# Part 3 of the MLP: its second matrix computed plainly instead of with seven products

## The chip, the cores and the metric

The kernel runs on one core of one Trainium2 chip. The metric is device time in microseconds (us), from the first instruction to the last; a lower number is better. The core has five engines that run side by side, each through its own queue in order: TensorE (PE in the rows; PEld is its loading of the stationary operand), VectorE (DVE), ScalarE (ACT), GpSimd (POOL) and SyncE (SP), which here only issues transfers. TensorE writes its sums into eight accumulators ("banks") of 128 x 512 numbers.

## The reference

Two layers work on 512 tokens of 1024 channels. Each layer has a mixer (sparse attention, gated linear attention and pooling side by side), a normalisation, the MLP and a second normalisation. Only the last two are touched:

```
D_MODEL, SEQ, D_FF = 1024, 512, 4096
for l in range(2):
    ...
    h = layer_norm(ALPHA * h + mixed @ w_out[l], ln1_g[l], ln1_b[l])
    ff = square(relu(h @ w_up[l])) @ w_down[l]
    h = layer_norm(ALPHA * h + ff, ln2_g[l], ln2_b[l])
```

All data are float32.

## The kernel before

**Precision.** A product of two float32 matrices is made of three matmuls: each operand is split into a high part (a copy that rounds, by ScalarE) and a low part (operand minus high part, by VectorE), and high x high, high x low and low x high are summed in one bank (`steps`, line 598). A weight tile of 128 x 1024 numbers is loaded by SyncE into a raw buffer (four of them, `NRAW`, and two more for "chained" tiles), then split into one of four pairs of buffers (`NSPL`, lines 385 to 443). A pair becomes free when the last matmul that reads it is done.

**The MLP in four parts.** `mlp` (line 1716) goes through the 4096 hidden channels in four parts `c` of 1024. In each part the first matrix makes 512 x 1024 activations, squares of relu, which are split into high and low; the second matrix multiplies them with 1024 rows of `w_down` and adds the result to `h`, four tiles of 128 tokens x 1024 channels. Part 0 does both plainly. Its second matrix is a loop over two halves of 512 output columns, over four pairs of weight rows j, over four token tiles t (lines 1770 to 1783): each weight tile is used by all four token tiles, then released, and four banks are open. It is 2 x 4 x 4 x 2 x 3 = 192 matmuls of 512 columns.

**Seven products.** In parts 1 to 3 both matrices are cut into quarters, and seven products of sums of quarters take the place of eight. For the first matrix this is `up_pair` (line 1519): pairs of 128-channel blocks, matmuls of 256 columns. For the second it is `down_seven` (line 1667), in the order of `STEPS` (line 1856). The activation quarters are A11, A12, A21, A22: the first digit is the half of the tokens, the second the even or odd block of 128 hidden channels. The sums S1 to S4 of activation quarters are made by `sums` (line 1592) on VectorE and split by `split_sums` (line 1652). The sums of weight quarters are made by transfers that add to a raw buffer, issued on GpSimd's queue (`accumulate`, line 358; eight in each part), each after the split of the sum before it (`group`, line 419). One part's second matrix is 7 products x 2 token tiles x 2 x 2 weight rows x 3 = 168 matmuls of 512 columns. Some products end in one bank and are added to `h` more than once: `out` (line 1673) adds a bank to a half of a token tile.

**What follows part 3.** When both halves of a token tile have had their last addition (and its statistics, `bn_stats`), `norm` (line 562) normalises it: aggregate on VectorE (mv), two small steps on GpSimd (rs, the reciprocal root), two passes with mv and two with rs on VectorE. In layer 0 TensorE then transposes the tile in two groups of four (`transpose_h`, line 536), ScalarE and VectorE split the result into hT, and layer 1 begins with block A, 96 matmuls of 400 columns, token tile by token tile, and block B. In layer 1 the normalised halves are transferred out.

**The order.** A planner in the kernel (`Planner`, line 35) writes out every engine's order before the program runs: it follows estimated costs (`pl.op`, `pl.pe`), lets one main generator issue matmuls and takes spawned generators (splits, additions, normalisations, transposes) as soon as its own clock says that what they need is ready. The chip then runs each queue in exactly that order.

Of the kernel before, what the change touches and what calls it, by code (L numbers as in the profile page):

```python
# [130 lines left out]
def trunk_kernel(ctx: ExitStack, tc, x, w_in, cmp_pos, cmp_w1, cmp_w2, gla_w_gate2, gla_b_gate,  # L131
# [151 lines left out]
    for l in range(depth):  # L283
# [36 lines left out]
        for c in range(4):  # L320
# [11 lines left out]
            if c == 0:  # L332
                dn = [[add_unit((2, 512), [(full, cols(w_down[l], 8 * c + 2 * j, 2, 512 * hf, 512))])
                       for j in range(4)] for hf in range(2)]
            else:
                dn = quarters(w_down[l], c)
# [302 lines left out]
    def layer_work(l, hT, nhT):  # L639
# [879 lines left out]
        def up_pair(i0, i1, ff, m, c):  # L1519
# [63 lines left out]
            def out12():  # L1583
# [6 lines left out]
                pl.spawn(sums(), 1)  # L1590
# [76 lines left out]
        def down_seven(ff, dn, c, stat):  # L1667
# [3 lines left out]
            seen = []  # L1671

            def out(n, number, i, t, hf, op, end, fin):
# [5 lines left out]
                if fin and c == 3:  # L1679
                    yield  # L1680
                    nc.vector.bn_stats(stat[t][:, hf, :], h[t][:, s])  # L1681
                    pl.op("dve", 0.6, [stat[t]], [h[t]])
                    seen.append(t)
                    if seen.count(t) == 2:
                        pl.spawn(norm(l + 1, t, stat[t], gb2, None if last else nhT), 1)
# [4 lines left out]
            for (name, src, n, _), (f, b, outs) in zip(SEVEN, STEPS):  # L1690
# [3 lines left out]
                t0, hf, op, end, fin = outs  # L1694
# [5 lines left out]
                for i, j in order:  # L1700
# [10 lines left out]
                    if j == 1:  # L1711
                        pl.spawn(out(b, count[b], i, t0 + i, hf, op, end, fin), 1)
# [3 lines left out]
        def mlp():  # L1716
            for c in range(4):
# [18 lines left out]
                else:  # L1736
                    ff = {n: [None] * 4 for n in ("A11", "A12", "A22", "S1", "S2", "S3", "S4", "raw")}
                    pl.spawn(split_sums(ff, c, 0), 3)
                    yield from up_pairs(up, ff, c)

                def ff_ready(k, t):
                    return E("ff", id(ffp[t // 2]), k // 2)

                def ff_parts(k, t):
                    c0 = 256 * (k % 2) + 128 * (t % 2)
# [15 lines left out]
                def done(ps, t, hf):  # L1761
                    y_part(ps, t, slice(512 * hf, 512 * hf + 512), True)
                    yield

                if c == 3:
                    drop(12)
                if c:
                    yield from down_seven(ff, dn, c, stat)
                    continue
                for hf in range(2):  # L1770
                    if True:
                        pss = []
                        for j in range(4):
                            for t in range(NT):
# [4 lines left out]
                                piece(pss[t], t, dn[hf][j], j)  # L1779
# [47 lines left out]
    def everything():  # L1827
# [3 lines left out]
        for l in range(depth):  # L1831
# [24 lines left out]
STEPS = (("A11", "e", (0, 0, OP.add, False, False)), ("S1", "b", (2, 1, OP.add, False, False)),  # L1856
         ("S2", "e", (0, 1, OP.subtract, False, False)), ("S4", "b", (0, 1, OP.add, True, True)),
# [59 lines left out]
```

## Time and profile before

| | us |
|---|---|
| median of 3 runs | 1214.7 |
| lowest, highest | 1212.32, 1216.29 |
| the profiled execution | 1213.42 |
| its span, first to last instruction | 1211.7 |
| TensorE busy | 1169.2 (96%) |
| VectorE busy | 1009.7 (83%) |
| ScalarE busy | 666.8 (55%) |
| GpSimd busy | 238.4 (20%) |
| mean granted clock of TensorE | 0.988 of full |

Times in the rows are counted from the start of the span. A matmul's end is modelled and overlaps the next one's start, so the distance of two starts is what one costs, not its length. A wait is put down to the engine and line that came last.

### The profile page before, as it was taken

To read this page: it belongs to the slowest core of one execution; us is meant where nothing else is said; L and a number is where in the kernel's file an instruction comes from. 1 tells how busy PE (TensorE), PEld (TensorE's weight loads), DVE (VectorE), ACT (ScalarE), POOL (GpSimd) and SP (SyncE) were. 2 spreads that over 40 slices of the span, in tenths; PEclk is the share of its full clock that TensorE was granted. 3 is DMA by queue.
4 is the path that set the end of the run, shared out by engine and by line. 5 is a ranking of instruction groups with operands and counts; after the bars stand their busy time and mean duration, and the time that the engine had idled before them with its cause. 6 is when DMAs were issued, how large, how long until landed. Compare 5 with 4: busy or idle time off the path is not lost.

```text
span 1211.7 us, 19153 instructions
## 1 busy us (share of the span) xinstructions
PE 1169.2 (96%) x7161; PEld 1025.5 (85%) x7161; DVE 1009.7 (83%) x1810; ACT 666.8 (55%) x1299; POOL 238.4 (20%) x301
## 2 busy tenths in 40 slices
PE   8999999999999999999899999999999999999995
PEld 7898788889889899797688987888998898988974
DVE  3799998897679799797867999988967897987978
ACT  4633666663348567386336435756633584774851
POOL 1255431210001201102212644302100011011021
PEclk9999999999999999999989998999999999999998
DMA  7514103153325836747634040131523358466482
GB/s 217 148 40 118 44 19 109 27 152 105 88 76 151 168 111 127 151 140 156 136 97 116 22 134 29 36 96 35 158 87 104 105 122 157 140 113 157 147 158 88
DMA packets 138317, 132.80 MB, mean 110 GB/s; under 512 B 17744, under 2 KB 104304, under 8 KB 138224
## 3 DMA queue, kind: packets, MB, share of 16 engines
q1 hardware_dynamic: 125168, 106.41, 29.6%
q0 software_dynamic: 13056, 25.17, 12.6%
q8 instruction: 56, 0.92, 0.3%
q14 instruction: 37, 0.30, 0.1%
HBM read 129.46 MB, written 2.10 MB: 109 GB/s over the span
## 4 chain that ended last, share of the span: by engine, by line
PE 67%; DVE 17%; DMA 8%; issue 4%; ACT 2%; POOL 2%; SPq 0%; DVEq 0%; POOLq 0%; ACTq 0%
PE b L181 64%; DMA wr<-in_w_down_dram 7%; DVE s L206 6%; DVE wl L206 3%; PE b L186 3%; DVE s L219 2%; DVE h L219 1%; DVE nb L223 1%; ACT s L194 1%; ACT wh L194 1%; DVE h L206 1%; POOL s L206 1%; POOL r L206 1%; DMA h<-in_x_dram 1%; DVE stats L1681 1%
## 5 line engine op out<-in xcount | busy, mean ns | idle before, releaser
L181 PE MATMUL b<-wh,s 128*128 128x512 f32 x1184 | 386.7, 399 | 5.1 <-DVE mv L564 2.2
L194 ACT ACTIVATE wh<-wr 128x1024 fp32r<-128x1024 f32 (+4 forms) x230 | 220.3, 969 | 217.2 <-PE b L181 126.7
L206 DVE TENSOR_TENSOR wl<-wr,wh 128x1024 fp32r<-128x1024 f32 (+4 forms) x222 | 251.8, 1140 | 96.5 <-ACT wh L194 95.6
L181 PEld LDWEIGHTS b<-wh,s 128*128 128x128 f32 x1184 | 222.9, 189 | 59.9 <-ACT wh L194 4.0
L194 ACT ACTIVATE s<-s 128x512 fp32r<-128x512 f32 (+7 forms) x424 | 216.0, 534 | 96.7 <-DVE s L206 75.8
L181 PE MATMUL b<-wl,s 128*128 128x512 f32 x592 | 234.6, 396 | 4.1 <-DVE wl L206 4.1
L194 ACT ACTIVATE s<-b 128x384 fp32r<-128x384 f32 (+6 forms) x270 | 121.4, 460 | 142.3 <-PE b L181 102.3
L206 DVE TENSOR_TENSOR s<-s,s 128x512 fp32r<-128x512 f32 (+6 forms) x302 | 183.7, 627 | 13.3 <-ACT s L194 7.1
L181 PE MATMUL b<-hTh,wh 128*128 128x256 f32 (+1 forms) x544 | 176.7, 325 | 3.1 <-ACT s L194 3.1
L181 PE MATMUL b<-hTh,wl 128*128 128x256 f32 (+1 forms) x544 | 174.6, 321 | 0.0
L181 PE MATMUL b<-hTl,wh 128*128 128x256 f32 (+1 forms) x544 | 174.2, 320 | 0.0
L360 POOL DMA_DIRECT2D wr<-in_w_down_dram x48 | 58.3, 1237 | 547.2 <-DVE wl L206 321.0
L181 PE MATMUL b<-s,s 128*128 128x256 f32 (+4 forms) x1008 | 143.7, 296 | 0.0
L181 PEld LDWEIGHTS b<-wl,s 128*128 128x128 f32 x592 | 111.7, 189 | 30.6 <-DVE wl L206 6.8
L181 PEld LDWEIGHTS b<-s,s 128*128 128x128 f32 (+1 forms) x1008 | 125.0, 191 | 2.3 <-issue 0.3
L206 DVE TENSOR_TENSOR s<-b,s 128x256 f32<-128x256 f32 (+8 forms) x206 | 100.4, 499 | 20.3 <-PE b L181 12.5
L181 PEld LDWEIGHTS b<-hTh,wh 128*128 128x128 f32 x544 | 102.5, 188 | 12.4 <-ACT s L194 4.3
L181 PEld LDWEIGHTS b<-hTh,wl 128*128 128x128 f32 x544 | 102.6, 189 | 8.5
L181 PEld LDWEIGHTS b<-hTl,wh 128*128 128x128 f32 x544 | 102.5, 189 | 8.1
L181 PE MATMUL b<-hTh,s 128*128 128x256 f32 x576 | 108.9, 283 | 0.0
L181 PEld LDWEIGHTS b<-hTh,s 128*128 128x128 f32 x576 | 91.7, 191 | 0.1
L181 PE MATMUL b<-hTl,s 128*128 128x256 f32 x288 | 81.4, 283 | 0.0
(151 smaller groups left out, 1686.6 us busy)
## 6 DMA issues: line engine op xcount, KB each, us to landing
wr<-in_w_up_dram SPq DMA_DIRECT2D x52, 512.0 KB, 4.4
wr<-in_w_down_dram SPq DMA_DIRECT2D x52, 512.0 KB, 4.4
wr<-in_w_down_dram POOLq DMA_DIRECT2D x48, 512.0 KB, 5.9
wr<-in_w_out_dram SPq DMA_DIRECT2D x20, 512.0 KB, 3.5
wr<-in_w_in_dram SPq DMA_DIRECT2D x24, 384.0 KB, 3.2
wr<-in_w_up_dram SPq DMA_DIRECT2D x24, 256.0 KB, 3.2
wr<-in_w_in_dram SPq DMA_DIRECT2D x8, 400.0 KB, 6.2
wr<-in_w_in_dram SPq DMA_DIRECT2D x6, 512.0 KB, 3.6
```

The source lines that it names most:

```text
L181: nc.tensor.matmul(o, a, b, start=start, stop=stop, **({"skip_group_check": True} if loose else {}))
L186: nc.tensor.transpose(o, a, i)
L194: nc.scalar.activation(o, a, func, scale=scale, **kw)
L206: e.tensor_tensor(out=o, in0=a, in1=b, op=op)
L219: nc.vector.scalar_tensor_tensor(o, a, s, b, op0=op0, op1=op1)
L223: nc.vector.tensor_reduce(o, a, axis=AX.X, op=op, negate=negate)
L360: nc.gpsimd.dma_start(o, a, accum_op=OP.add)
L1681: nc.vector.bn_stats(stat[t][:, hf, :], h[t][:, s])
```

## The change

In part 3 alone, of both layers, the second matrix is computed as in part 0, with 192 matmuls instead of 168; parts 1 and 2 keep the seven products, and the first matrix of part 3 does too. The eight weight tiles of part 3 are loaded and split as they are: no tile is "chained", and no transfer adds to one. Of the activations the quarter A21 itself is kept and split (in `out12`), and their sums are not made. The first half of the output columns goes pair of weight rows by pair of weight rows over four open banks, as in part 0. The second half goes token tile by token tile: tile t takes all four weight tiles one after the other, so all four stay in the split buffers until tile 3 has used them. Behind each tile of the second half comes its normalisation at once (`done`). The additions to `h` carry the statistics in part 3.

```diff
--- before.py
+++ after.py
@@ -329,7 +329,7 @@
                     up.append([add_unit((8, 128), [(full, cols(w_up[l], 0, 8, 1024 * c + 128 * m, 128))])])
                     if c and m % 2:
                         pairs[up[-1][0]] = up[-2][0]
-            if c == 0:
+            if c in (0, 3):
                 dn = [[add_unit((2, 512), [(full, cols(w_down[l], 8 * c + 2 * j, 2, 512 * hf, 512))])
                        for j in range(4)] for hf in range(2)]
             else:
@@ -1587,7 +1587,16 @@
                 yield
                 act(x_, x_, AF.Relu)
                 act(x_, x_, AF.Square)
-                pl.spawn(sums(), 1)
+                if c < 3:
+                    pl.spawn(sums(), 1)
+                    return
+                f = slot(dt=F32R)
+                act(f[:, lo_], x_)
+                yield
+                tt(f[:, hi_], x_, f[:, lo_], OP.subtract)
+                ff["A21"][m // 2] = f[:, lo_], f[:, hi_]
+                drop(3)
+                ev("ff", c, "A21", m // 2)
 
             def sums():
                 yield [key("C11"), key("X1")]
@@ -1664,25 +1673,17 @@
                     ff[n][p] = fh[:, s_], fl[:, s_]
                     ev("ff", c, n, p)
 
-        def down_seven(ff, dn, c, stat):
+        def down_seven(ff, dn, c):
 
 
             ps = {}
-            seen = []
-
-            def out(n, number, i, t, hf, op, end, fin):
+
+            def out(n, number, i, t, hf, op, end):
                 s = slice(512 * hf, 512 * hf + 512)
                 tt(h[t][:, s], h[t][:, s], ps[n][i], op)
                 if end:
                     free()
                 ev("down", c, n, number, i)
-                if fin and c == 3:
-                    yield
-                    nc.vector.bn_stats(stat[t][:, hf, :], h[t][:, s])
-                    pl.op("dve", 0.6, [stat[t]], [h[t]])
-                    seen.append(t)
-                    if seen.count(t) == 2:
-                        pl.spawn(norm(l + 1, t, stat[t], gb2, None if last else nhT), 1)
                 yield
 
             count = {"a": 0, "b": 0, "e": 0}
@@ -1691,7 +1692,7 @@
                 if not count[b]:
                     yield [("bank", 2)]
                     ps[b] = [bank(), bank()]
-                t0, hf, op, end, fin = outs
+                t0, hf, op, end = outs
                 keys = [(dn[src][j], n) for j in range(2)]
                 if f in ("A12", "S3", "A22"):
                     order = [(i, j) for i in range(2) for j in range(2)]
@@ -1709,7 +1710,7 @@
                     if i == 1:
                         used(keys[j])
                     if j == 1:
-                        pl.spawn(out(b, count[b], i, t0 + i, hf, op, end, fin), 1)
+                        pl.spawn(out(b, count[b], i, t0 + i, hf, op, end), 1)
                 drop({"A11": 4, "S1": 0, "S2": 8, "S3": 8, "S4": 0, "A12": 0, "A22": 8}[f])
                 count[b] += 1
 
@@ -1734,14 +1735,22 @@
                         yield from early_up(m, 1, ffp, acc)
                     ev("upped")
                 else:
-                    ff = {n: [None] * 4 for n in ("A11", "A12", "A22", "S1", "S2", "S3", "S4", "raw")}
-                    pl.spawn(split_sums(ff, c, 0), 3)
+                    ff = {n: [None] * 4 for n in ("A11", "A12", "A21", "A22", "S1", "S2", "S3", "S4", "raw")}
+                    if c < 3:
+                        pl.spawn(split_sums(ff, c, 0), 3)
                     yield from up_pairs(up, ff, c)
 
+                def quarter(k, t):
+                    return "A" + "12"[t // 2] + "12"[k % 2]
+
                 def ff_ready(k, t):
+                    if c:
+                        return E("ff", c, quarter(k, t), k // 2)
                     return E("ff", id(ffp[t // 2]), k // 2)
 
                 def ff_parts(k, t):
+                    if c:
+                        return [a[:, 128 * (t % 2):128 * (t % 2) + 128] for a in ff[quarter(k, t)][k // 2]]
                     c0 = 256 * (k % 2) + 128 * (t % 2)
                     return [a[:, c0:c0 + 128] for a in ffp[t // 2][k // 2]]
 
@@ -1758,17 +1767,37 @@
                         a, b = ff_parts(k, t)
                         passes(ps, a, b, wh[:, kk, :], wl[:, kk, :], k == 0, k == 7)
 
-                def done(ps, t, hf):
-                    y_part(ps, t, slice(512 * hf, 512 * hf + 512), True)
+                def done(ps, t, hf, c=c, stat=stat):
+                    y_part(ps, t, slice(512 * hf, 512 * hf + 512), c == 0, stat[t][:, hf, :] if c == 3 else None)
                     yield
+                    if c == 3 and hf == 1:
+                        yield from norm(l + 1, t, stat[t], gb2, None if last else nhT)
 
                 if c == 3:
                     drop(12)
-                if c:
-                    yield from down_seven(ff, dn, c, stat)
+                if c in (1, 2):
+                    yield from down_seven(ff, dn, c)
                     continue
+
+                def piece_steps(ps, t, ui, j):
+                    wh, wl = parts[ui]
+                    for kk in range(2):
+                        k = 2 * j + kk
+                        a, b = ff_parts(k, t)
+                        yield from steps(ps, a, b, wh[:, kk, :], wl[:, kk, :], k == 0, k == 7)
+
                 for hf in range(2):
-                    if True:
+                    if c == 3 and hf == 1:
+                        for t in range(NT):
+                            yield [("bank", 1)]
+                            ps = bank()
+                            for j in range(4):
+                                yield [("split", dn[hf][j])]
+                                yield from piece_steps(ps, t, dn[hf][j], j)
+                                if t == NT - 1:
+                                    used(dn[hf][j])
+                            pl.spawn(done(ps, t, hf), 1)
+                    else:
                         pss = []
                         for j in range(4):
                             for t in range(NT):
@@ -1776,7 +1805,10 @@
                                 if j == 0:
                                     yield [("bank", 1)]
                                     pss.append(bank())
-                                piece(pss[t], t, dn[hf][j], j)
+                                if c:
+                                    yield from piece_steps(pss[t], t, dn[hf][j], j)
+                                else:
+                                    piece(pss[t], t, dn[hf][j], j)
                                 if j == 3:
                                     pl.spawn(done(pss[t], t, hf), 2)
                             used(dn[hf][j])
@@ -1853,10 +1885,10 @@
 LAND = 5.5
 SEVEN = (("P1", "B11", 0, False), ("P5", "B11", 1, False), ("P6", "B11", 2, False), ("P3", "B22", 0, False),
          ("P2", "B21", 0, True), ("P7", "B22", 1, True), ("P4", "B11", 3, True))
-STEPS = (("A11", "e", (0, 0, OP.add, False, False)), ("S1", "b", (2, 1, OP.add, False, False)),
-         ("S2", "e", (0, 1, OP.subtract, False, False)), ("S4", "b", (0, 1, OP.add, True, True)),
-         ("A12", "a", (0, 0, OP.add, True, True)), ("S3", "e", (2, 1, OP.subtract, False, True)),
-         ("A22", "e", (2, 0, OP.add, True, True)))
+STEPS = (("A11", "e", (0, 0, OP.add, False)), ("S1", "b", (2, 1, OP.add, False)),
+         ("S2", "e", (0, 1, OP.subtract, False)), ("S4", "b", (0, 1, OP.add, True)),
+         ("A12", "a", (0, 0, OP.add, True)), ("S3", "e", (2, 1, OP.subtract, False)),
+         ("A22", "e", (2, 0, OP.add, True)))
 NATT = (6, 8)
 NEARLY = 2
 KEEP = 6
```

## Rows read from the trace of the kernel before

**Rows 1.** The page, part 1: busy time, share and instructions of TensorE.

```profile
PE 1169.2 (96%) x7161; PEld 1025.5 (85%) x7161; DVE 1009.7 (83%) x1810; ACT 666.8 (55%) x1299; POOL 238.4 (20%) x301
```

**Rows 2.** TensorE timeline (start, length, instruction): part 0's plain stage and what follows.

```profile
309.31 0.40 PE L181 MATMUL b<-wh,s 128*128 128x512 f32 x1
...
353.97 0.28 PE L181 MATMUL b<-hTh,wh 128*128 128x256 f32 x1
```

**Rows 3.** TensorE timeline, layer 0: part 3's seven products, first and last.

```profile
555.75 0.39 PE L181 MATMUL b<-wh,s 128*128 128x512 f32 x1
...
602.39 0.39 PE L181 MATMUL b<-wh,s 128*128 128x512 f32 x1
```

**Rows 4.** TensorE's waits, 555 to 603 us: releaser, total, times, longest.

```profile
PE b L181 <- DVE wl L206: 1.8, 2, 1.0
PE b L181 <- DVE mv L564: 1.5, 1, 1.5
PE b L181 <- ACT s L194: 0.8, 1, 0.8
PE b L181 <- DVE s L206: 0.5, 1, 0.5
```

**Rows 5.** TensorE timeline, layer 1: part 0's start, part 3's first and last.

```profile
910.45 0.40 PE L181 MATMUL b<-wh,s 128*128 128x512 f32 x1
...
1156.59 0.40 PE L181 MATMUL b<-wh,s 128*128 128x512 f32 x1
...
1199.09 0.39 PE L181 MATMUL b<-wh,s 128*128 128x512 f32 x1
```

**Rows 6.** TensorE timeline between the layers: tile 0's transposes, block B's start.

```profile
603.68 0.66 PE L186 MATMUL b<-ident,h 128*128 128x128 f32 x4 [0.91 <-DVE h L219]
607.48 1.11 PE L186 MATMUL b<-ident,h 128*128 128x128 f32 x4 [3.15 <-DVE h L219]
...
631.20 0.40 PE L181 MATMUL b<-hTh,wh 128*128 128x512 f32 x1
```

**Rows 7.** One stretch: length, busy us of five engines, granted clock, DMA, GB/s.

```profile
608.20:612.40 4.20, 4.05 (x14) 3.40 (x13) 4.20 (x7) 1.00 (x2) 1.52 (x2) 0.50 0.24 63
```

**Rows 8.** TensorE timeline, block A of layer 1: transposes, matmuls.

```profile
614.77 0.60 PE L186 MATMUL b<-ident,h 128*128 128x128 f32 x4
...
615.40 0.34 PE L181 MATMUL b<-wl,hTh 128*128 128x400 f32 x1
...
618.85 0.34 PE L181 MATMUL b<-wh,hTh 128*128 128x400 f32 x1
...
623.60 0.34 PE L181 MATMUL b<-wh,hTl 128*128 128x400 f32 x1
```

**Rows 9.** Timeline of VectorE behind layer 1's last matmul.

```profile
1200.58 0.64 DVE L206 TENSOR_TENSOR h<-h,b 128x512 f32<-128x512 f32 x1
...
1201.80 0.69 DVE L1681 BATCH_NORM_STATS2 stats<-h 128x6 f32<-128x512 f32 x1
...
1203.05 0.20 DVE L564 BATCH_NORM_AGGREGATE mv<-stats 128x2 f32<-128x12 f32 x1
...
1205.78 1.41 DVE L219 SCALAR_TENSOR_TENSOR h<-h,mv,s 128x512 f32<-128x512 f32 x2
1207.10 1.41 DVE L219 SCALAR_TENSOR_TENSOR h<-h,rs,s 128x512 f32<-128x512 f32 x2
```

**Rows 10.** Timeline of VectorE, layer 0: splits of 1024 columns in parts 0 and 3.

```profile
332.93 1.23 DVE L206 TENSOR_TENSOR wl<-wr,wh 128x1024 fp32r<-128x1024 f32 x1 [0.17 <-ACT wh L194]
...
592.68 1.18 DVE L206 TENSOR_TENSOR wl<-wr,wh 128x1024 fp32r<-128x1024 f32 x1
```

**Rows 11.** Timeline of GpSimd: steps of the reciprocal root, layer 0 and layer 1.

```profile
592.87 1.08 POOL L212 TENSOR_SCALAR rs<-mv 128x1 f32<-128x1 f32 x1 [14.46 <-DVE mv L564]
...
1200.76 0.22 POOL L212 TENSOR_SCALAR rs<-mv 128x1 f32<-128x1 f32 x1 [5.77 <-DVE mv L564]
...
1204.03 0.92 POOL L206 TENSOR_TENSOR rs<-rs,mhalf 128x1 f32<-128x1 f32 x1
```

## The prediction

> **What bounds the kernel now.** TensorE is busy in 96% of the span [rows 1], and nearly all of it at one matmul after the other, so the first question of any change here is how many matmuls it adds and how many gaps it closes. The share alone can't answer that; the places can. I looked at the order of TensorE's work in three kinds of stretch, then at its waits in them, then at VectorE after the last matmul.
>
> Plain second matrix, as part 0 has it: the 192 matmuls of 512 columns of layer 0 begin at 309.31 and the next stage begins at 353.97 [rows 2]: 44.66 us, 0.2326 us each, with no wait listed between. That is the pitch of this matmul when nothing holds it.
>
> Seven products, as part 3 has it: the stage holds 7 x 2 x 2 x 2 x 3 = 168 matmuls of the same form, 39.1 us at that pitch. In layer 0 it runs from 555.75 to 602.39 + 0.23 = 602.62 [rows 3], 46.9 us: 7.8 us are lost. The waits there [rows 4] add up to 4.6 us and have four causes: the split of a weight sum that is late, an accumulator that is not yet taken up, and sums of activations that ScalarE and VectorE still make (the row that names mv stands behind the addition to h that frees the accumulator). The rest is lower pace behind those waits. In layer 1 the same 168 run from 1156.59 to 1199.09 + 0.23 [rows 5], 42.7 us: 3.6 us lost.
>
> Behind the stage of layer 0 comes the normalisation of all four token tiles, their transposes and block A of layer 1 (96 matmuls of 400 columns). The reader is to see the two gaps before transposes that wait for the normalised tile, 0.91 and 3.15 us, that block A comes only behind the second, and that block B starts at 631.20 [rows 6]: 28.6 us from the last matmul of part 3. [...] At full pace block A's matmuls are (623.60 - 618.85) / 26 = 0.183 us apart, and a group of four transposes adds 615.40 - 614.77 - 0.18 = 0.45 us [rows 8]. So the work there is 96 x 0.183 + 8 x 0.45 = 21.1 us, and I allow 0.3 us for the small transposes of the parameters: 21.4. 7.2 us of the 28.6 are lost.
>
> Behind the stage of layer 1 comes only VectorE: it finishes at 1207.10 + 1.41 = 1208.51 [rows 9], 9.4 us after the start of the last matmul, because the tails of tiles 0 to 3 lie on it one behind the other.
>
> **The change, part by part.** All sums are against the profiled execution, 1213.42 us with a span of 1211.7; the median of the runs shown is 1214.7, 1.3 above it, and I carry the difference over to the median.
>
> Matmuls. 168 become 4 x 2 x 8 x 3 = 192 in each layer, 24 x 0.2326 = 5.6 us of TensorE more. With the gaps of the old stage gone this gives 44.7 - 46.9 = -2.2 us in layer 0 and 44.7 - 42.7 = +1.9 us in layer 1. The stage in the trace that is nearest is part 0's plain one, which has no gap in either half, but the new second half differs: it goes tile by tile, so it wants its fourth pair of weight rows after 18 matmuls, 4.2 us into the half, not after 72. There are four split buffers; the fourth becomes free only when the first half ends. In part 0 the same split ends on VectorE at 332.93 + 1.23 = 334.16 [rows 10], when the second half had begun at about 309.31 + 96 x 0.2326 = 331.64: 2.5 us. The margin is 1.7 us; a bn_stats that now also follows the last additions of the first half can take some 0.7 of it. Cost 0, bound 1.5 us per layer if another split slips in.
>
> What goes: per layer six splits of 1024 columns on ScalarE and VectorE, six additions to h, the sums of the activations and their splits, and eight adding transfers on the queue of GpSimd. None of it is on TensorE. It is what the four waits of [rows 4] wait for, so it is counted there and not a second time. The transfers on the queue of SyncE grow from six to eight of the same size, and all are due at a rate of one in 24 x 0.2326 = 5.6 us; beside them the queue has only the four loads of gain and bias and, behind, the next layer's first weights. What comes: one split of 256 columns per pair of blocks (A21), needed only after 84 matmuls, 19.5 us into the stage. Cost 0 for both; without that cover they cost one ScalarE pass and one subtraction, under 2 us.
>
> From part 3 to layer 1. Before, tiles 0 and 1 got their last addition with the fifth product and tiles 2 and 3 with the seventh, and VectorE had their normalisation between additions, statistics and splits of 1024 columns, most of it behind the last matmul. Now tile 0 is complete 3 x 24 matmuls = 16.7 us before the end, tile 1 11.2 us, tile 2 5.6 us. One tile needs, on VectorE, 0.64 + 0.69 + 0.20 + 1.41 + 1.41 = 4.35 us [rows 9] and two subtractions of transposed halves, about 0.64 each: 5.6 us by durations, about 5.1 since neighbours overlap by some 0.08. That fits into 5.6, and no weight split can fall between before the last tile, since all four split buffers are held. So tiles 0 and 1 are transposed and ready before the stage ends and block A can start at once. The eight groups of transposes remain, four of them now inside part 3. The gain is 7.2 us at most. What can take some of it back: the planner puts a transpose into TensorE's queue when it thinks the tile is normalised, and everything queued behind waits with it, as it did for 0.91 and 3.15 us [rows 6]. It counts 0.6 us for a pass that takes 0.66 to 0.7, and some 0.5 us for the two steps on GpSimd that make the reciprocal root, where 1204.03 + 0.92 - 1203.25 = 1.7 us pass [rows 9, 11]. I take 0.75 us for each of the two tiles that it can hit inside part 3: 1.5 us, nearest to the 0.91 row; bounds 0 and 7.2. So -5.7 us. The first weights of block A are also split later, since the buffers come free 4.2, 2.8, 1.4 and 0 us before the end; the fourth is wanted 18 matmuls, 3.3 us, after it, and costs about 2 us. Cost 0.
>
> The end. After layer 1's last matmul only tile 3 is left: its addition, statistics, aggregate and four passes, 4.35 us by durations, about 4.0 with the overlaps, plus 0.44 from the matmul's start to its end and the signal, plus what the passes with rs wait for GpSimd. The two steps on GpSimd took 1.7 us there while the two passes with mv take 1.3, so 0.4; bounds 0 and 0.8. VectorE ends about 4.85 us after the start of the last matmul, not 9.4: -4.6 us, between -4.2 and -5.0. What follows it (the last transfer out) is the same.
>
> How long one step on GpSimd takes depends on its neighbour: the same operation on one column took 1.08 us at 592.87 and 0.22 at 1200.76 [rows 11]. [...]
>
> Sum: -2.2 - 5.7 + 1.9 - 4.6 = -10.6 us. 1213.42 becomes 1202.8 (span 1201.1), and the median 1214.7 becomes 1204.1.
>
> **Rivals.** (a) The transition is not won. VectorE's work for a tile, 5.1 to 5.6 us, nearly fills the 5.6 us of a tile's matmuls, and in the last tile four splits of block A's weights come in between. If that piles up, block A waits as it does now: only 1.5 us or none of the 7.2 is gained, the sum is about -4.9 and the median 1209.8, and with gaps in the second half up to 1212. For it: how full VectorE is. Against it: block A goes tile by tile, 4.4 us each, and needs tile 2 only 8.8 us and tile 3 13 us after the end.
>
> (b) Slower. The transposes of the four tiles of layer 0 stand in TensorE's queue too early, and each holds back the matmuls behind it. Before, no transpose stood between the matmuls of part 3, so a wait there is new. [...] It decides from 10.6 + 3.6 = 14.2 us in all, 3.5 us per tile. The longest wait of this kind in the trace is 3.15 us, with four tiles piled up; the estimates are wrong by about 1 us. [...]
>
> (c) The planner's changed times reorder the mixers of layer 1, with a loss of 3 to 8 us: 1207 to 1212. Against it: from the start of part 0's plain stage to that of part 3's the two layers take 555.75 - 309.31 = 246.44 and 1156.59 - 910.45 = 246.14 us [rows 2, 3, 5], so the order is steady against different beginnings, at least in that stretch.
>
> **How the numbers follow.** Forecast 1204.1 with its own range 1201 to 1208: 0.70. (a) 0.17, of which 0.10 faster and 0.07 within 0.3% (3.6 us, about what a measurement of this kernel can tell from no change). (b) 0.06, slower. (c) 0.07, of which 0.03 faster and 0.04 within. Faster 0.83, same 0.11, slower 0.06. The range reaches from all gains in full with a fast run (1214.7 - 2.2 - 7.2 + 1.9 - 5.0 = 1202.2, less 1.7 for the spread of the runs: 1200.5) to most of (a), 1210.5.
>
> **What would show it.** [...] Wrong: a wait before the transposes above 2 us, a gap 4.2 us into the second half, a clock of 0.5 in block A, or a layer 1 whose stretch from block B to part 0 is longer than before.

## The result, and the profile after

The changed kernel takes 1206.6 us (median; 1204.64 to 1207.74) beside 1213.0 for the kernel before (1212.32 to 1216.29), both measured in turn: a ratio of 0.9942, interval 0.993 to 0.9955, 6.4 us less by the medians. The forecast was 1204.1, its range 1200.5 to 1210.5. The profiled execution of after took 1205.97 us, with a span of 1204.2, against 1213.42 and 1211.7: 7.5 us less, where 10.6 were forecast. All sums below are in these spans.

The kernel is faster although TensorE has 48 matmuls more. The page of after, part 1 (busy us, share, instructions); [rows 1] has the line of before:

```profile
PE 1169.2 (97%) x7209; PEld 1028.1 (85%) x7209; DVE 974.1 (81%) x1746; ACT 649.0 (54%) x1279; POOL 221.9 (18%) x285
```

TensorE's busy sum did not move at all: the two stages hold 8.5 us more of it (42.22 and 40.03 before, 46.20 and 44.58 after), the transition 4.7 us less (24.40 before, 19.72 after, with 17 instructions fewer and a granted clock of 1.00 where it was 0.88), and the stretches ahead of the two stages 3.8 us less with the same matmuls. The other three engines lost 36, 18 and 17 us of work, which buys nothing by itself: the first experiment has the same relief and is slower than before. What moved is seen in TensorE's timeline of after (start, length, instruction, and in brackets the wait before it), at the places of [rows 3, 5, 6]:

```profile
556.91 0.40 PE L181 MATMUL b<-wh,s 128*128 128x512 f32 x1
...
589.81 0.60 PE L186 MATMUL b<-ident,h 128*128 128x128 f32 x4
...
602.91 0.39 PE L181 MATMUL b<-wh,s 128*128 128x512 f32 x1
603.14 0.34 PE L181 MATMUL b<-wh,hTh 128*128 128x400 f32 x1
...
615.80 0.24 PE L186 MATMUL b<-ident,s 64*128 64x64 f32 x1 [2.43 <-DMA s<-in_cmp_pos_dram]
...
625.25 0.39 PE L181 MATMUL b<-hTh,wh 128*128 128x512 f32 x1
...
1151.07 0.40 PE L181 MATMUL b<-wh,s 128*128 128x512 f32 x1
...
1195.42 0.39 PE L181 MATMUL b<-wh,s 128*128 128x512 f32 x1
```

The plain stage of layer 0 runs from 556.91 to 603.14, 46.2 us with four groups of transposes in it (the first is the line at 589.81). Block A follows the last matmul by one pitch. No transpose waits; the one wait of the transition is a 2.43 us one for a small parameter tile, in the middle of block A's work. Layer 1's stage is 44.58 us, 192 x 0.2322. Its windows say the same (stretch; length, then busy us of PE, PEld, VectorE, ScalarE and GpSimd with counts, granted clock, DMA share, GB/s). First the two stages, then the beginning of block A:

```profile
556.90:603.20 46.30, 46.30 (x211) 37.69 (x210) 28.47 (x42) 11.54 (x17) 5.88 (x9) 1.00 0.24 73
1151.00:1195.70 44.70, 44.70 (x194) 35.94 (x193) 25.78 (x37) 6.69 (x10) 5.11 (x6) 1.00 0.17 61
603.10:608.50 5.40, 5.40 (x31) 5.36 (x31) 5.37 (x10) 1.44 (x3) 1.52 (x2) 1.00 0.55 134
```

TensorE is busy in the whole of all three, and the granted clock is 1.00, where [rows 7] had 0.50 in block A.

The tail, as VectorE's timeline of after shows it, where [rows 9] had some eight microseconds of work of several tiles:

```profile
1195.84 0.69 DVE L206 TENSOR_TENSOR h<-h,b 128x512 f32<-128x512 f32 x1 [0.58 <-PE b L181]
1196.57 0.69 DVE L1354 BATCH_NORM_STATS2 stats<-h 128x6 f32<-128x512 f32 x1
1197.29 0.21 DVE L564 BATCH_NORM_AGGREGATE mv<-stats 128x2 f32<-128x12 f32 x1
1197.54 1.41 DVE L219 SCALAR_TENSOR_TENSOR h<-h,mv,s 128x512 f32<-128x512 f32 x2
1199.41 1.42 DVE L219 SCALAR_TENSOR_TENSOR h<-h,rs,s 128x512 f32<-128x512 f32 x2 [0.46 <-POOL rs L206]
```

Only tile 3 is left; VectorE ends at 1200.83, 5.41 us after the start of the last matmul (before: 9.42). From there to the end of the span it is 3.37 us (before: 3.19).

The span, stretch by stretch:

| stretch | before | after | moved | forecast |
|---|---|---|---|---|
| start to part 3's second matrix, layer 0 | 555.75 | 556.91 | +1.16 | 0 |
| that stage, layer 0 | 46.87 | 46.23 | -0.64 | } |
| its end to block B of layer 1 | 28.58 | 22.11 | -6.47 | } -7.9 together |
| block B to part 3's second matrix, layer 1 | 525.39 | 525.82 | +0.43 | 0 |
| that stage, layer 1 | 42.73 | 44.58 | +1.85 | +1.9 |
| end of the last matmul to the end of the span | 12.38 | 8.55 | -3.83 | -4.6 |
| sum | 1211.70 | 1204.20 | -7.50 | -10.6 |

Stage and transition of layer 0 must be taken together, -7.11, since four of the eight groups of transposes moved from the second into the first. Within the first stretch, 0.78 us is the first-matrix stage of part 3 (40.62 to 41.40) and 0.45 the seven products of part 2 (40.72 to 41.17); part 2's stage lay between 39.99 and 41.17 in all the kernels that leave it alone, so the 0.45 is not put down to the change. Within the fourth stretch, the first-matrix stage of part 3 is again longer, 40.65 to 41.41, the mixers (block B to part 0) are not: 279.25 and 279.20.

### The profile page after: what moved, and what is told of

It is laid out like the page before. It is cut to its first block, busy times and chain, and to the rows that moved or that the text cites. A ratio compares the mean times of both kernels' runs of the same rounds, so it can differ in the third digit from the quotient of the medians.

```text
span 1204.2 us, 19123 instructions
## 1 busy us (share of the span) xinstructions
PE 1169.2 (97%) x7209; PEld 1028.1 (85%) x7209; DVE 974.1 (81%) x1746; ACT 649.0 (54%) x1279; POOL 221.9 (18%) x285
## 4 chain that ended last, share of the span: by engine, by line
PE 76%; DVE 13%; DMA 4%; ACT 2%; issue 2%; POOL 2%; SPq 1%; POOLq 0%; DVEq 0%; ACTq 0%
PE b L181 74%; DVE s L206 4%; DMA wr<-in_w_down_dram 3%; PE b L186 2%; DVE s L219 2%; ACT s L194 1%; DVE nb L223 1%; DVE wl L206 1%; ACT wh L194 1%; SPq L345 1%; POOL r L206 1%; DVE h L219 1%; POOL s L206 1%; DMA h<-in_x_dram 1%; DVE s L212 0%
## 5 line engine op out<-in xcount | busy, mean ns | idle before, releaser
L181 PE MATMUL b<-wh,s 128*128 128x512 f32 x1216 | 394.0, 398 | 0.5 <-ACT s L194 0.5
L206 DVE TENSOR_TENSOR wl<-wr,wh 128x1024 fp32r<-128x1024 f32 (+4 forms) x210 | 237.5, 1135 | 114.0 <-ACT wh L194 113.0
L194 ACT ACTIVATE wh<-wr 128x1024 fp32r<-128x1024 f32 (+4 forms) x218 | 208.7, 964 | 211.1 <-PE b L181 150.4
L181 PEld LDWEIGHTS b<-wh,s 128*128 128x128 f32 x1216 | 228.2, 188 | 53.1 <-ACT wh L194 1.0
L194 ACT ACTIVATE s<-s 128x512 fp32r<-128x512 f32 (+7 forms) x416 | 209.5, 528 | 92.6 <-DVE s L206 71.9
L181 PE MATMUL b<-wl,s 128*128 128x512 f32 x608 | 240.1, 395 | 1.8 <-DVE wl L206 1.8
L206 DVE TENSOR_TENSOR s<-s,s 128x512 fp32r<-128x512 f32 (+7 forms) x278 | 170.6, 629 | 13.5 <-ACT s L194 7.5
L181 PEld LDWEIGHTS b<-wl,s 128*128 128x128 f32 x608 | 114.4, 188 | 27.8 <-DVE wl L206 3.0
L360 POOL DMA_DIRECT2D wr<-in_w_down_dram x32 | 38.9, 1229 | 399.5 <-DVE s L206 219.8
```

Of the source, the lines that this page charges most:

```text
L181: nc.tensor.matmul(o, a, b, start=start, stop=stop, **({"skip_group_check": True} if loose else {}))
L194: nc.scalar.activation(o, a, func, scale=scale, **kw)
L206: e.tensor_tensor(out=o, in0=a, in1=b, op=op)
L360: nc.gpsimd.dma_start(o, a, accum_op=OP.add)
```

## The experiments

The theory to be tested: the gain is made behind the two stages, by the order of the output tiles, which hides tail and transposes under TensorE's work; the plain stage by itself only trades 5.6 us of matmuls for gaps. The rival: the gaps and the load of the other engines (weight sums, adding transfers) were the cost, and the order is a detail.

**The plain stage without the order.** After, its second half as in part 0:

```diff
                 for hf in range(2):
-                    if c == 3 and hf == 1:
+                    if False:
                         for t in range(NT):
```

> The changed kernel with one part undone: the second half of part 3's columns goes pair of weight rows by pair of weight rows over four open banks, like the first half; all else stays. Theory (the two gains have two causes: the plain stage closes the stage's gaps, the tile-by-tile order alone moves normalisation ahead of the end): the stage stays at 44.6 us of matmuls in both layers; in layer 1 VectorE ends 13 to 16 us after the start of the last matmul, not 5.4, since four tiles of 4.4 to 5 us begin within the last 4.2 us; from part 3's last matmul to block B 25 to 29 us, not 22.1. Median 1206.6 + 8 to 10 + 3 to 7 = 1217 to 1224, slower than the kernel before. Rival (taking the weight sums off VectorE is what frees it, the order matters little): at most 1209.

Measured: 1219.9 us, ratio to before 1.0061 (1.0046 to 1.0076), slower than the kernel before, and 13.6 us of span above after. The stages are 44.52 and 44.59 us, with no gap. What follows them is, in TensorE's timeline behind layer 0's stage (last matmul, transposes, block A), then VectorE's behind layer 1's (last matmul started at 1201.83), then the window behind layer 0's stage:

```profile
600.64 0.40 PE L181 MATMUL b<-wh,s 128*128 128x512 f32 x1
605.88 1.97 PE L186 MATMUL b<-ident,h 128*128 128x128 f32 x8 [4.84 <-DVE h L219]
609.78 0.36 PE L186 MATMUL b<-ident,s 64*128 64x64 f32 x1 [1.93 <-DMA s<-in_cmp_pos_dram]
610.07 0.70 PE L181 MATMUL b<-wh,hTh 128*128 128x400 f32 x1
```

```profile
1202.97 0.69 DVE L1354 BATCH_NORM_STATS2 stats<-h 128x6 f32<-128x512 f32 x1
...
1212.99 1.41 DVE L219 SCALAR_TENSOR_TENSOR h<-h,rs,s 128x512 f32<-128x512 f32 x2
```

```profile
600.90:610.00 9.10, 2.33 (x10) 1.75 (x9) 9.07 (x17) 2.67 (x5) 6.89 (x13) 0.64 0.47 102
```

In 9.1 us TensorE works 2.3, and VectorE all of them. Block A starts 9.2 us after the last matmul, at first at a slower pace (its first matmuls are 0.33 us apart, not 0.183; the granted clock is 0.64 in that window and 0.81 in the 10 us behind it), and block B 31.1 us after it (after: 22.11). At the end VectorE ends 12.57 us after the start of the last matmul (after: 5.41). The difference to after is the transition +9.0, the stage of layer 0 -1.7 (its transposes are outside now), the tail +7.2, what lies ahead of layer 0's stage -0.6, the rest -0.3: 13.6. The theory holds; the tail (12.57) is a little under its bounds of 13 to 16, the transition (31.1) above its 25 to 29, and 1.93 us of that is again the wait for the parameter tile. The rival falls: gap-free stages with relieved engines and no order are worth less than nothing.

**The one wait that is left.** After, with the three lines that load the position parameters moved ahead of the other opening loads:

```diff
             yield [("raw", u[ORDER[0]][-1])]
+            pv_ = cmp_pos[l].rearrange("a r d -> (a r) d")
+            dma(posr[:, 0:64], pv_)
+            dma(posr[:, 64:128], pv_)
...
-            pv_ = cmp_pos[l].rearrange("a r d -> (a r) d")
-            dma(posr[:, 0:64], pv_)
-            dma(posr[:, 64:128], pv_)
```

> The changed kernel with the two transfers of the compression positions issued first among the small transfers that open a layer, not last. Theory (block A has caught up with them: TensorE waits 2.4 us for that transfer before a small transpose, where the kernel before came to the same place later): the wait goes, block B of layer 1 starts 2.4 us earlier, median 1204.2. Rival (the wait is only the last of several, block A or B is held by the next thing, such as the first weights of block B): block B at the same time within 0.5 us, median 1206.6.

In after, SyncE issues the opening loads from 604.32 on, and reaches this one at 613.07 (timeline of SyncE):

```profile
604.32 0.99 SPq L345 DMA_DIRECT2D bg<-in_gla_b_gate_dram  x2
...
613.07 1.23 SPq L345 DMA_DIRECT2D s<-in_cmp_pos_dram  x2
```

In the kernel before it issues it at 610.07, and the transposes that use it, at 613.37, have no wait: there block A starts at 608.25, 5.1 us later than in after, and the load 3.0 us earlier. Measured with the lines moved: 1203.2 us, ratio to before 0.9924 (0.9908 to 0.9941), span 1201.0, and the transposes at 612.90 without a wait, block B at 622.38:

```profile
612.90 0.27 PE L186 MATMUL b<-ident,s 64*128 64x64 f32 x1
...
622.38 0.39 PE L181 MATMUL b<-hTh,wh 128*128 128x512 f32 x1
```

The transition is 19.64 us, 2.47 less than in after, the stages the same. Block A's work, with the four groups of transposes that remain there, is by [rows 8] 96 x 0.183 + 4 x 0.45 = 19.4 us: the wait of 2.43 us was nearly all that the new transition still lost.

**The seven products without their weight sums.** Before, the eight adding transfers of part 3 left out (its weight sums are not formed; splits and matmuls stay as many):

```diff
             else:
                 dn = quarters(w_down[l], c)
+                if c == 3:
+                    bare.update(dn["B11"] + dn["B22"])
...
         def add(i, n):
-            accumulate(raws[i], adds[i][n])
+            if i not in bare:
+                accumulate(raws[i], adds[i][n])
```

> The kernel before with the eight transfers that add to a weight tile left out in part 3 (so the weight sums are not made there; the same tile is split again, all splits and matmuls stay). Theory W (the gaps of the seven-product stage come from weight sums that land and are split late): the stage of layer 0 falls from 46.9 to 42 to 44 us, that of layer 1 from 42.7 to 40 to 41, the waits for a split of weights are gone, the transition and the end stay; median 1213 less 5 to 7. Rival S (the gaps come from the sums of activations): both stages within 1 us of before, median 1211 to 1214.

Measured: 1203.3 us, ratio 0.9923 (0.9908 to 0.9937). Windows of the two stages in this kernel, and the same in the kernel before:

```profile
556.40:596.30 39.90, 39.22 (x171) 31.48 (x169) 34.99 (x50) 17.67 (x22) 2.51 (x4) 1.00 0.21 60
1150.50:1190.40 39.90, 39.22 (x170) 31.30 (x168) 35.07 (x51) 14.99 (x19) 2.51 (x4) 1.00 0.04 14
```

```profile
555.70:602.70 47.00, 42.37 (x170) 31.95 (x169) 35.02 (x49) 18.75 (x23) 10.10 (x10) 0.96 0.69 140
1156.50:1199.40 42.90, 40.23 (x171) 31.13 (x169) 34.99 (x50) 16.16 (x20) 10.10 (x10) 1.00 0.61 117
```

39.9 us for 168 matmuls, 0.8 above their pitch, in both layers, though VectorE is as busy as before (35.0). So with the chain of a weight sum gone (split, adding transfer into the raw buffer, next split) nearly all that the seven products lose in part 3 is gone too; in layer 0 the granted clock is 1.00 then where it was 0.96 before, which is within the gain. The run also takes the traffic of these transfers away (DMA share 0.21 and 0.04, from 0.69 and 0.61) and doesn't tell it from the chain. The direction was as the theory had it, the size (9.4 us of the median) above its 5 to 7; and that VectorE's load alone were the cause falls.

The chain doesn't have to cost this. Part 1 of the kernel before has the same 168 matmuls and the same eight adding transfers, and its stage takes 38.92 us in layer 0 and 38.97 in layer 1, with no wait (TensorE's timeline of before, layer 0, the stage's first matmul and the first behind it):

```profile
394.90 0.39 PE L181 MATMUL b<-wh,s 128*128 128x512 f32 x1
...
433.82 0.28 PE L181 MATMUL b<-hTh,wh 128*128 128x256 f32 x1
```

Part 2 takes 40.72 and 40.59 with one wait of 0.8. In layer 0 GpSimd issues the first adding transfer 10.3 us ahead of part 1's stage, but 6.7 us ahead of those of parts 2 and 3, and beside part 3's come the loads of gain and bias. This points at when the chain starts and at what comes in beside it, not at its length; seven products in part 3 with an earlier chain were not tried. The run also sets a bound: seven products whose weight sums cost nothing, with the exposed transition (28.5 us) and the tail behind the last matmul (11.3 us, 12.4 before), only come to where the plain stage with the moved parameter loads already is, 1203.2.

**The seven products without their activation sums.** Before, the four subtractions and additions of the quarters skipped in part 3 (their sums are not formed, the splits remain):

```diff
-                tt(s1, A11, A21, OP.subtract)
-                tt(A21, A21, A22, OP.subtract)
-                yield
-                tt(A11, A21, A11, OP.subtract)
-                yield
-                tt(U2, A12, A11, OP.add)
+                if c < 3:
+                    ...
```

> The kernel before with the four additions on VectorE that make the sums of activations left out in part 3 (their splits stay and take what lies in the tiles). Theory W (weight sums carry most of the gaps): the two waits for a split sum of activations, 1.3 us, and the pace at the lower clock behind them go: the stage of layer 0 falls by 2 to 4 us, that of layer 1 by 1 to 1.5; median 1213 less 3 to 5. Rival S (activation sums carry them): the stage of layer 0 falls by over 5 us and that of layer 1 by over 2.5, to about 40 to 41 us each.

Measured: 1207.2 us, ratio 0.9951 (0.9936 to 0.9966). Layer 0's stage 43.30 us (-3.57), layer 1's 42.92 (+0.2). In layer 0, of the two waits that named an activation (the last two rows of [rows 4]) one is gone and one is down from 0.5 to 0.2 us (TensorE's waits, 555 to 604 us; the first line is the transposes behind the stage):

```profile
PE b L186 <- DVE h L219: 3.5, 1, 3.5
PE b L181 <- DVE mv L564: 2.3, 1, 2.3
PE b L181 <- DVE wl L206: 0.8, 1, 0.8
PE b L181 <- DVE s L206: 0.2, 1, 0.2
```

The expectation holds for layer 0's stage and fails for layer 1's: there the waits for these sums (0.7 and 0.5) and for a weight split (0.8) go too, but the one for an accumulator grows from 0.7 to 2.1 us, and the granted clock of the stage is 0.96. The median falls by 5.5 us, above the 3 to 5 expected. The run doesn't keep the two causes apart: without the sums of activations the chain of weight sums runs ahead as well, its third adding transfer is issued at 555.37, 0.5 us ahead of the stage, where before it came 6.3 us into it. So the 7.0 us without the weight sums and the 3.6 without those of the activations overlap; together they are more than the 7.8 lost.

**Part 2 plain as well.** After, with part 2 treated as part 3 (its second half in the old order):

```diff
-            if c in (0, 3):
+            if c in (0, 2, 3):
...
-                if c < 3:
+                if c < 2:
...
```

> The changed kernel with part 2's second matrix computed plainly as well (pair of weight rows by pair of weight rows in both halves, the first half's loop; part 1 alone keeps the seven products there). Theory (the seven products lose to the plain form only where gaps eat their 5.6 us and where the end of the layer stands behind them; part 2's stage of seven products takes 41.2 and 40.3 us in the two layers): part 2's stage becomes 44.7 us in both layers, nothing else gains: median 1206.6 + 7 to 8 = 1214. Rival (seven products never pay here, since they load ScalarE, VectorE and the transfers of the whole stretch around them): other stages get shorter by as much, median at most 1206.6.

Measured: 1215.4 us, ratio 1.0029 (1.0017 to 1.004), 8.8 us over after. Part 2's second matrix takes 44.65 us in both layers where the seven products took 41.17 and 40.29 in after, 7.8 in sum, and its first-matrix stage is longer by 0.76 and 0.81. In layer 0 (TensorE's timeline, start of the stage and of the next):

```profile
475.05 0.40 PE L181 MATMUL b<-wh,s 128*128 128x512 f32 x1
...
519.70 0.28 PE L181 MATMUL b<-hTh,wh 128*128 128x256 f32 x1
```

The theory holds. The plain form that gains in part 3 loses in part 2, because behind part 2's second matrix stands the next first matrix, which needs nothing of it: there is no exposed work to hide. The price per stage, 3.5 to 4.4 us, is 5.6 us of matmuls less what gaps there were.

**The gain and bias loads a little later.** Before, the four loads of the next gain and bias (1 MB) moved, in the planner's order, from the end of part 3's first-matrix stage to behind step S4 of its seven products:

```diff
+                if c == 3 and f == "S4":
+                    pl.spawn(load_gb(l + 1, ln2_g[l], ln2_b[l], gb2), 0)
...
-                    pl.spawn(load_gb(l + 1, ln2_g[l], ln2_b[l], gb2), 0)
```

> The kernel before with one thing moved: the four loads of gain and bias of the last normalisation are issued behind the fourth product of part 3, not at the end of its first-matrix stage. Theory C (the first adding transfer of part 3 lands after 10.4 us where part 2's lands after 5.9, because 1 MB of gain and bias arrives with it, and the chain of weight sums stays late from there): it lands in about 6 us, the stage of seven products falls from 46.9 to 42 to 44 us in layer 0 and from 42.7 to 41 to 42 in layer 1, median 1213 less 3 to 6. Rival (the chain of split, transfer, split is too long without that): the stage within 1 us of before, median 1211 to 1214.

Measured: 1211.2 us, ratio 0.9992 (0.9979 to 1.0004). Layer 0's stage is 44.77 us (-2.1), layer 1's 42.97. The third adding transfer is issued at 559.12 us instead of 562.04 (timeline of GpSimd, before and with the loads later), with stages that start 0.4 us apart:

```profile
562.04 1.20 POOL L360 DMA_DIRECT2D wr<-in_w_down_dram  x1 [7.86 <-DVE wl L206]
```

```profile
559.12 1.20 POOL L360 DMA_DIRECT2D wr<-in_w_down_dram  x1 [4.56 <-DVE wl L206]
```

The same four waits stand in the stage, the weight sum's among them, 1.5 us where [rows 4] had 1.8, and no gain in time can be told from none.

This doesn't settle what the loads cost, because the edit hardly moved them on the chip. SyncE issued them from 552.73 on, 3.4 us ahead of the stage, where before it was from 549.35 on, 6.4 us ahead; the end of S4 would have been 96 matmuls, over 22 us, into it. The second adding transfer, issued at 553.35, still came in beside them: its split waits for it until 562.47, 9.1 us, where before it was 9.9 and in part 2, without such loads, at most 6.0 (timelines of SyncE and ScalarE, loads later):

```profile
552.73 0.89 SPq L345 DMA_DIRECT2D s<-in_ln_g_dram  x2
...
562.47 1.06 ACT L194 ACTIVATE wh<-wr 128x1024 fp32r<-128x1024 f32 x1 [3.11 <-DMA wr<-in_w_down_dram]
```

3 us less of overlap were worth 2.1 us in layer 0 and nothing in layer 1. Whether loads that are truly out of the way would close the rest was not tried.

**The copies of A21 held back.** The params-first version, with the copy of A21's high part made to wait until the pair is complete and ScalarE is free:

```diff
                 f = slot(dt=F32R)
+                yield [key("C11"), free_act]
                 act(f[:, lo_], x_)
```

> The run with the compression positions first, and beside it the split of the quarter A21 put behind a wait for ScalarE to be free in the planner's clock, so that it is not queued at once behind relu and square. Theory (0.78 us that the first-matrix stage of part 3 lost in each layer is a copy for the seventh product that stands behind A21's third pass on ScalarE): that stage falls from 41.4 to 40.6 us in each layer, median 1203.2 - 1.5 = 1201.7. Rival (the copy stands behind the earlier weight splits): 41.4 us as now, 1203.2.

This is about the 0.78 us in the first matrix of part 3. After has two waits of 0.5 us before its last blocks, before and this version one (TensorE's waits from 514 us to the stage's end; after, then this version):

```profile
PE b L181 <- ACT s L194: 1.0, 2, 0.5
```

```profile
PE b L181 <- ACT s L194: 0.5, 1, 0.5
```

In after ScalarE's timeline shows what came in front: a weight copy of 1.05 us, then passes of the activations:

```profile
549.22 1.05 ACT L194 ACTIVATE wh<-wr 128x1024 fp32r<-128x1024 f32 x1
550.17 1.30 ACT L194 ACTIVATE s<-s 128x256 f32<-128x256 f32 x3
551.38 0.36 ACT L194 ACTIVATE s<-b 128x256 f32<-128x256 f32 x1
```

Measured: 1202.7 us, ratio 0.9924 (0.991 to 0.9938). The first-matrix stage is 40.95 and 40.91 us, half of the way back (40.6 was expected). The other half has another cause: without its weight sums the kernel before is also longer here, 41.53 and 41.61, with no A21 to split. What the two kernels share is that the weights of the second matrix wait for no adding transfer, so their copies can come earlier on ScalarE's queue, ahead of the passes that the last blocks of the first matrix need. That this is the other half was argued, not tried alone. By time, this version can't be told from the one without the hold; both beat the two kernels of this case.

## Why the prediction was right, and where it missed

Right in sign and mechanism, 3.1 us too far in size by the spans, 4.2 by the medians (6.4 of 10.6). The time lies in the likeliest case's own range, 1201 to 1208, and of the rivals none came. That it lies in there is partly luck: the forecast started from 1214.7, and the kernel before took 1213.0 when both were measured in turn. From there the same sum gives 1202.4, and the range moved with it, 1199.3 to 1206.3, ends just short of the measured 1206.6 (the wide range, to 1208.8 then, still holds it).

*The stages.* Layer 1: +1.9 forecast, +1.85 measured. Layer 0: 44.7 forecast, which with four groups of transposes at 0.45 us [rows 8] is 46.5; 46.23 measured. The plain second half in the new order has no gap; the fourth split of it ended at 582.49, 3.2 us after the half's start at 579.3 where 4.2 were allowed (VectorE's timeline of after; the half's start is the stage's plus 96 x 0.233):

```profile
581.28 1.21 DVE L206 TENSOR_TENSOR wl<-wr,wh 128x1024 fp32r<-128x1024 f32 x1
```

The margin of 1.7 us shrank to 1.0, as its 0.7 for bn_stats said.

*What the old stage lost.* The prediction named four waits and took them at 4.6 us plus "lower pace behind those waits". The run without weight sums shows that 7.0 of the 7.8 us in layer 0 and 2.8 of the 3.6 in layer 1 go when the adding transfers of part 3 are left out, though only 1.8 us of the waits in layer 0 named a split of weights. The list of waits was a poor measure of causes; the sum needed only the stage's length, so nothing followed from it.

*The transition.* -5.7 forecast. With the transposes counted where they are now, -7.11 against -7.9 for stage and transition: 0.8 short. The failed step is "I take 0.75 us for each of the two tiles": the transposes in TensorE's queue waited for nothing at all, so the 1.5 us belong to 0. In their place 2.43 us are lost to the parameter tile, whose load the prediction didn't count; it has only "I allow 0.3 us for the small transposes of the parameters". Its load had been covered by the very gap that was to be closed: block A moved ahead by 5.1 us, and the queue that feeds it fell behind by 3.0. The move of three lines got back 2.47. (The 21.1 us of work in the prediction's sum is 21.2 by its own terms; nothing hangs on it.)

*The first matrix of part 3.* "Cost 0 for both; without that cover they cost one ScalarE pass and one subtraction, under 2 us." It cost 0.78 + 0.76 us. The step asked when the last A21 is needed (late, 19.5 us into the next stage) and not what stands behind its copy on ScalarE's queue in the meantime: the passes that free an accumulator for the last blocks. About half of it is that copy; the rest is lost without it too, in the kernel before without weight sums.

*The tail.* -4.6 forecast, -3.83 measured: 5.41 us from the last matmul, not 4.85. "4.35 us by durations, about 4.0 with the overlaps" was wrong: addition, statistics and aggregate of one tile each need the one before, and they did not overlap: 0.73 and 0.72 us from start to start, at 0.69 us of length. In the timeline that [rows 9] is from, the statistics at 1201.80 stood between passes of another tile (1201.13 and 1202.40). Another 0.18 us of the miss lies behind VectorE's end, which the prediction took as the same. The wait for rs was 0.46, as the 0.4 said; the two GpSimd steps took 0.77 and 0.92 us:

```profile
1197.59 0.77 POOL L212 TENSOR_SCALAR rs<-mv 128x1 f32<-128x1 f32 x1 [3.78 <-DVE mv L564]
1198.45 0.92 POOL L206 TENSOR_TENSOR rs<-rs,mhalf 128x1 f32<-128x1 f32 x1
```

In these traces the time of the first step goes with what VectorE does beside it: 0.77 us beside the passes with mv at 1197.54, 1.08 beside the subtraction of two weight tiles at 592.68 [rows 10, 11], and 0.22 beside the addition of an accumulator at 1200.58 [rows 9, 11], as once more in before at 603.83. Why it does was not shown.

*The rivals.* (a) VectorE was full at the start of block A (5.37 of 5.40 us), as the rival said, but TensorE did not wait for it: block A followed by one pitch. (b) No transpose waited. (c) The mixers of layer 1 took 279.20 us, 279.25 before. Miss in all: 0.8 (transition) + 1.5 (first matrix) + 0.8 (tail) = 3.1 us; what is left (0.45 in part 2, -0.4 elsewhere) cancels.

## What to carry to other kernels

A saving of multiplications must be weighed against what stands behind its stage: here 5.6 us of TensorE per layer were worth paying because the plain form lets output tiles finish one by one and so hides normalisation and transposes (13.6 us by the run without the order), while in part 2, with nothing exposed behind it, the plain form costs 8.8 us. Order the last stage before a serial epilogue so that each output tile is done as early as its neighbours allow. And when a gap is to be closed, list everything that the gap had been covering, the small loads and the other engines' queues too, for the next wait is among them: three moved lines were worth another 2.5 us of the transition.

The comparison holds against the seven products as they stood in part 3. Two ways to keep them were not tried: a chain of weight sums that starts earlier, as in part 1, and an order of the products that finishes the output tiles one by one.

## What the runs showed of the hardware

In these rows neighbours on VectorE overlap where they don't depend on each other, and not where they do. In after's layer 0 an addition of another tile starts 0.61 us after a statistics pass of 0.69 us (578.04, 578.65); in the tail each next step needs the last and starts 0.73 and 0.72 us after it:

```profile
578.04 0.69 DVE L1354 BATCH_NORM_STATS2 stats<-h 128x6 f32<-128x512 f32 x1
578.65 0.67 DVE L206 TENSOR_TENSOR h<-h,b 128x512 f32<-128x512 f32 x1
579.36 0.69 DVE L1354 BATCH_NORM_STATS2 stats<-h 128x6 f32<-128x512 f32 x1
```

(578.65 to 579.36 is again a dependent pair, 0.71.) An addition doesn't hold back every neighbour by that much: in the kernel before one is followed by a pass of another tile, and that one starts 0.59 us after it:

```profile
1195.44 0.68 DVE L206 TENSOR_TENSOR h<-h,b 128x512 f32<-128x512 f32 x1
1196.03 0.74 DVE L219 SCALAR_TENSOR_TENSOR h<-h,rs,s 128x512 f32<-128x512 f32 x1
```

So the serial chain of this tail is summed by full durations, a stream of such independent steps by their pitch. The additions of 512 columns in these lines take 0.67 to 0.69 us (one operand is an accumulator), the statistics 0.69; the dependent pairs start 0.71 to 0.73 us apart, the independent ones 0.59 and 0.61, which hides some 0.1 us of a step.

The small loads were not free for the queue that issues them: in after the 16 opening loads of layer 1 take SyncE from 604.32 to 614.30, 0.6 us each on average, so the issue of the last one ends 10 us after that of the first begins.

A transfer that adds into its destination was issued by GpSimd in 1.20 us, and the split that waits for it stands behind issue and landing: the first one of part 3 in layer 0, issued at 549.04, was split from 559.42 on. The eight of part 3 cost its seven products 7.0 us in layer 0 and 2.8 in layer 1, more than the 5.6 us of matmuls that they save in layer 0 and half of them in layer 1; the eight of part 1 cost nothing that shows (38.92 and 38.97 us).
